# Seven-product matmuls of the second block: four products in one PSUM chain, sets interleaved by two products, scratch loads into idle weight pages

## The chip, the cores and the metric

One core of one Trainium2 chip runs the whole program: a gated attention block and, behind it, a second block with a short convolution and a SwiGLU. The metric is device microseconds (us) of one execution. Three runs of the kernel before gave 2760.71, 2763.57 and 2766.59 us.

## The reference, cut to what matters

Only the second block is touched. `x` is 1024 tokens by 1024 features; everything is float32.

```python
def short_conv_mixer(h, w_in, conv_w, w_out, on_grid):
    gate_b, gate_c, hv = jnp.split(h @ w_in, 3, axis=-1)
    u = gate_c * hv
    conv = conv3_grid(u, conv_w) if on_grid else conv3_seq(u, conv_w)
    return (gate_b * conv) @ w_out

def swiglu(h, w_in, w_out):
    gate, up = jnp.split(h @ w_in, 2, axis=-1)
    return (jax.nn.silu(gate) * up) @ w_out

x = x + g1 * short_conv_mixer(modulate(rmsnorm(x, norm1_g), sh1, sc1), ...)
x = x + g2 * swiglu(modulate(rmsnorm(x, norm2_g), sh2, sc2), ffn_w_in, ffn_w_out)
return rmsnorm(x, final_g)
```

`h @ conv_w_in` is 1024x1024 by 1024x3072, `@ conv_w_out` 1024x1024 by 1024x1024, `@ ffn_w_in` 1024x1024 by 1024x5632, `@ ffn_w_out` 1024x2816 by 2816x1024.

## The kernel before, in words

**Seven products.** Each of the four matrix products is done by Strassen's scheme in Winograd's form: operands in two by two blocks, seven block products P1 to P7 in place of eight, and sums before and after. Each float32 operand is split into a rounded half `hi` and a rest `lo` (line 106, a cast on ScalarE, then line 107, a subtraction on VectorE), and a block product is hi·hi + hi·lo + lo·hi. For four blocks of 128 of the contraction that makes 12 matmuls of 128x512, called a product below.

**Into features (`seven`, lines 1266 to 1291).** The tokens are the right operand. Seven forms of them (B11, B21, B12, T1 to T4) lie split in seven slots of `H` (slots 0 to 4) and `HB` (slots 5 and 6). A *set* is 128 features of each of two column blocks of the weight: `left_operands` (1195) loads two 512 KB tiles through the ring of raw tiles (four buffers, `next_raw`; line 1215), forms the sums on VectorE (1233 to 1238) and splits them into the ring of four weight pages `W` (`w_177` to `w_180`) and one half of `PA`. A set has four PSUM banks, and the next set the other four. ScalarE copies P1 out of its bank (1273), P2 is then added to P1 in the bank, P3 to P5 and P4 to P7, and VectorE makes five additions that read PSUM (lines 1280, 1282, 1284, 1288, 1290). The convolution has 12 sets, the SwiGLU 22 (NFF); for four of the first five of the one and the first six of the other, P1 and P2 were made in advance (`ahead`, 1258) while the tokens were still being prepared. Called *late* here are the 24 other sets.

**Out of features (`out_products`, 1352).** The roles turn: the left operand is the features' forms (TC or TF, stored to DRAM scratch by `spill`, 1294), the right one the weight (P1, P2, P4) or sums of its blocks (P3, P5, P6, P7; `sums_steps`, 1316, makes them on GpSimd with loads and stores, one step or more after each set: `mix.tick`). All operands are loaded 512 KB at a time through the raw tiles and split into pages of the token slots, which are free by then. A product name covers four token groups t = 0 to 3 in four banks; P1, P2, P5, P3 use banks 0 to 3, the others 4 to 7. After each name `conv_use` (1505) or `ffn_use` (1586) takes the four banks over.

**Between the two.** `third` (1485) is called by the conv's P4 for tokens t and by P3 for tokens 4 + t: it normalizes (1493), transposes on TensorE through PSUM (1404), stores and reloads half of it, and makes the SwiGLU's seven token forms (`right_operands`, 1173). It takes two or three raw tiles per call. At the very end `fourth` (1579) normalizes and stores the output; the lines 1605 to 1618 belong to the last two product names.

**What sets the order.** Each engine runs its instructions in one order, and that is set when the program is built, by a list scheduler that follows the program's order and a simulated timeline. The DMA issues of SyncE are in such an order too, so a load that waits for a raw tile holds up those queued behind it.

Of the kernel before, what the change touches and what calls it, by code (L numbers as in the profile page):

```python
# [27 lines left out]
def program(tc, I, out):  # L28
# [4 lines left out]
    with ctx:  # L33
# [1110 lines left out]
        def U(i, n=1):  # L1144
            return E[:, i * 512:(i + n) * 512]
# [13 lines left out]
        ORDER = ("P1", "P6", "P5", "P7", "P2", "P3", "P4")  # L1159
# [40 lines left out]
        def left_operands(w, c1, c2):  # L1200
# [3 lines left out]
            st = dict(i=i, bank=4 * (i % 2), w={})  # L1204
# [8 lines left out]
            def load(c):  # L1213
# [4 lines left out]
            def half(p, o):  # L1218
                return [p.r[:, q * 1024 + o:q * 1024 + o + 512].rearrange("p (k n) -> p k n", k=4) for q in range(2)]

            def first(keep=True):
                r = load(c1)
                if keep:
                    st["r"] = r, load(c2)
                p = page()
                split(p.r[:, 0:1024], p.r[:, 1024:2048], p.f[:, 0:1024], r)
                st["w"].update(P1=half(p, 512), P2=half(p, 0))

            def rest():
                r1, r2 = st["r"] if "r" in st else (load(c1), load(c2))  # L1230
                split(pa[:, 0:512], pa[:, 512:1024], paf[:, 0:512], r2[:, 0:512])
                a11, a12, a21, a22 = r1[:, 0:512], r1[:, 512:1024], r2[:, 0:512], r2[:, 512:1024]
                V.tensor_tensor(a21, a22, a21, ALU.add)
                V.tensor_tensor(a22, a12, a22, ALU.subtract)
                p = page()
                split(p.r[:, 0:1024], p.r[:, 1024:2048], p.f[:, 0:1024], r2)
                V.tensor_tensor(a12, a21, a12, ALU.subtract)
                V.tensor_tensor(a11, a11, a12, ALU.subtract)
                q = page()
                split(q.r[:, 0:1024], q.r[:, 1024:2048], q.f[:, 0:1024], r1)  # L1240
                st["w"].update(P5=half(p, 0), P7=half(p, 512), P3=half(q, 0), P6=half(q, 512),
# [24 lines left out]
        def seven(st, where, units, c12):  # L1266

            early = "c11" in st
            if not early:
                st["first"]()  # L1270
                st["p1"] = units.get()
# [399 lines left out]
```

## Time and profile before

| | |
|---|---|
| three runs, median (lowest to highest) | 2763.57 us (2760.71 to 2766.59) |
| the profiled execution: time, span | 2762.01 us, 2760.2 us |
| mean granted TensorE clock in it | 0.969 |
| matmuls on TensorE, busy | 13582, 2575.8 us (93%) |
| VectorE, ScalarE, GpSimd busy | 1922.2, 1067.2, 652.1 us |
| the chain that ended last, by engine | PE 71%, DVE 10%, DMA 9%, ACT 4% |

PE is TensorE, DVE VectorE, ACT ScalarE, POOL GpSimd, SP SyncE, which issues the DMAs. The busy shares are means over the whole span. What a part of the change is worth must be read in its own stage, by what TensorE waits for there. The second block's stages are: the convolution's products into features, 1677 to 1895 us; out of features, 1895 to 1970; the transition with `third`, 1970 to 2085; the SwiGLU's products into features, to 2509; out of features, to 2737; and the tail without any matmul to 2760.2.

### The profile page before, as it was taken

What the parts mean: (1) busy time and instruction counts of PE and PEld (TensorE: products, weight loads), DVE (VectorE), ACT (ScalarE), POOL (GpSimd) and SP (SyncE); (2) the same over time, 40 slices, a digit from 0 to 9 for tenths busy, and PEclk for the clock granted to TensorE, in tenths of its full rate; (3) what the DMA queues carried; (4) which work ended last, traced back from release to release, by engine and by line L of the source; (5) the groups of instructions that cost most, each with busy time, mean ns of one, the idle gap of its engine ahead of it and who ended that gap; (6) DMA issues with size and microseconds to landing.
All of it is one profiled execution on the core that took longest, in us unless ns stands there. A gap on an engine that the chain in (4) does not pass through costs nothing.

```text
span 2760.2 us, 36848 instructions
## 1 busy us (share of the span) xinstructions
PE 2575.8 (93%) x13582; PEld 2202.0 (80%) x13582; DVE 1922.2 (70%) x3097; ACT 1067.2 (39%) x1887; POOL 652.1 (24%) x638
## 2 busy tenths in 40 slices
PE   8999999999999999999999968999677998999976
PEld 5799998879999778888898856777556786888865
DVE  5677776667778764556778958786766887775536
ACT  4333334323233544355557853223442222224333
POOL 2100000010003304123447740240221445210012
PEclk9999999999999999999999989999788999999988
DMA  7454343555445336442543233465533677426645
GB/s 257 145 143 118 97 127 122 153 168 156 127 117 153 124 113 198 153 133 71 194 156 123 92 118 96 129 221 172 178 114 108 197 245 233 156 96 212 197 143 175
DMA packets 336937, 416.44 MB, mean 151 GB/s; under 512 B 17830, under 2 KB 200638, under 8 KB 336242
## 3 DMA queue, kind: packets, MB, share of 16 engines
q1 hardware_dynamic: 329012, 403.08, 46.1%
q10 hardware_dynamic: 7744, 11.01, 1.1%
q8 instruction: 106, 1.74, 0.3%
q14 instruction: 75, 0.61, 0.1%
HBM read 320.12 MB, written 93.91 MB: 150 GB/s over the span
## 4 chain that ended last, share of the span: by engine, by line
PE 71%; DVE 10%; DMA 9%; ACT 4%; issue 3%; POOL 3%; SPq 0%; DVEq 0%; POOLq 0%; ACTq 0%
PE PS L516 16%; PE PS L1254 14%; PE PS L1376 8%; PE PS L603 7%; PE PS L676 5%; PE PS L392 5%; PE PS L1053 3%; PE PS L998 2%; PE PS L861 2%; PE PS L895 2%; PE PS L883 2%; DVE w L107 1%; PE PS L497 1%; DMA E<-in_ffn_w_out 1%; DMA raw<-in_a_w_in 1%
## 5 line engine op out<-in xcount | busy, mean ns | idle before, releaser
L1254 PE MATMUL PS<-H,w 128*128 128x512 f32 x1776 | 432.5, 400 | 42.5 <-ACT w L106 21.7
L1254 PEld LDWEIGHTS PS<-H,w 128*128 128x128 f32 x1776 | 340.9, 193 | 123.8 <-ACT w L106 25.9
L106 ACT CAST w<-raw 128x1024 fp32r<-128x1024 f32 x202 | 211.1, 1050 | 509.5 <-PE PS L1254 134.4
L107 DVE TENSOR_TENSOR w<-raw,w 128x1024 fp32r<-128x1024 f32 x200 | 268.0, 1344 | 138.7 <-ACT w L106 138.3
L516 PE MATMUL PS<-H,w 128*128 128x320 f32 x2112 | 320.5, 309 | 1.3 <-DVE TT L525 1.3
L516 PEld LDWEIGHTS PS<-H,w 128*128 128x128 f32 x2112 | 310.8, 188 | 3.3 <-DVE TT L525 1.5
L1376 PE MATMUL PS<-H 128*128 128x512 f32 x924 | 220.1, 397 | 29.7 <-ACT H L106 29.7
L107 DVE TENSOR_TENSOR H<-raw,H 128x1024 fp32r<-128x1024 f32 (+1 forms) x133 | 165.0, 1248 | 117.8 <-ACT H L106 115.4
L1376 PEld LDWEIGHTS PS<-H 128*128 128x128 f32 x924 | 176.9, 192 | 69.6 <-ACT H L106 30.9
L106 ACT CAST H<-raw 128x1024 fp32r<-128x1024 f32 (+1 forms) x133 | 134.1, 1018 | 212.0 <-DMA raw<-in_a_w_in 71.3
L339 POOL TENSOR_TENSOR H<-ACC,H 128x256 fp32r<-128x256 f32 x52 | 50.6, 973 | 609.7 <-ACT H L338 483.4
L1254 PE MATMUL PS<-HB,w 128*128 128x512 f32 x672 | 169.5, 404 | 23.0 <-ACT E L1273 13.2
L1254 PEld LDWEIGHTS PS<-HB,w 128*128 128x128 f32 x672 | 127.0, 191 | 58.6 <-ACT E L1273 14.4
L320 DVE SCALAR_TENSOR_TENSOR ACC<-raw,CO,ACC 128x512 f32<-128x512 f32 x182 | 134.3, 750 | 20.7 <-DMA raw<-in_ada_w 18.1
L516 PE MATMUL PS<-H 128*128 128x320 f32 x960 | 144.7, 309 | 0.0
L516 PEld LDWEIGHTS PS<-H 128*128 128x128 f32 x960 | 141.1, 188 | 0.5
L603 PE MATMUL PS<-w,H 128*128 128x512 f32 x600 | 140.0, 391 | 0.0
L107 DVE TENSOR_TENSOR PTR<-PS,PTR 128x512 fp32r<-128x512 f32 x176 | 106.2, 613 | 35.0 <-ACT PTR L106 33.7
L603 PEld LDWEIGHTS PS<-w,H 128*128 128x128 f32 x600 | 111.5, 188 | 23.3
L392 PE MATMUL PS<-H 128*128 128x512 f32 x510 | 120.9, 391 | 0.0
L870 ACT ACTIVATE s<-s,sm 128x641 f32<-128x641 f32 (+1 forms) x128 | 103.3, 807 | 42.3 <-DVE sm L868 41.7
L106 ACT CAST PTR<-PS 128x512 fp32r<-128x512 f32 x176 | 91.8, 524 | 54.4 <-PE PS L883 49.8
(342 smaller groups left out, 4881.2 us busy)
## 6 DMA issues: line engine op xcount, KB each, us to landing
raw<-in_a_w_in SPq DMA_DIRECT2D x96, 512.0 KB
raw<-in_ada_w SPq DMA_DIRECT2D x80, 512.0 KB
raw<-in_ffn_w_in SPq DMA_DIRECT2D x50, 512.0 KB
E<-in_ffn_w_out SPq DMA_DIRECT2D x66, 256.0 KB
raw<-in_a_w_out SPq DMA_DIRECT2D x32, 512.0 KB
raw<-in_conv_w_in SPq DMA_DIRECT2D x28, 512.0 KB
TFT<-E SPq DMA_DIRECT2D x44, 256.0 KB
SFS<-E SPq DMA_DIRECT2D x44, 256.0 KB
```

What stands on the lines that cost most here:

```text
L106: A.copy(hi, src)
L107: turn["split"] = (eng or V).tensor_tensor(lo, src, hif, ALU.subtract)
L320: V.scalar_tensor_tensor(ACC[:, s, :], r[:, j, :], CO[:, c, k:k + 1], ACC[:, s, :], ALU.mult, ALU.add)
L392: T.matmul(ps, HT[0][:, k, ap, t * 128:(t + 1) * 128], w[:, k % 2, :], start=k == 0 and n == 0, stop=k == 7 and n == 2)
L516: T.matmul(pss[h][:, 0:320], w[:, k, :], HT[0][:, k, ap, h * 320:(h + 1) * 320], start=k == 0 and n == 0, stop=k == 7 and n == 2)
L603: turn["mm"] = T.matmul(accs[t], ys[j].r[:, ap * 640 + t * 128:ap * 640 + (t + 1) * 128], wv[:, j, :], start=kp == 0 and j == 0 and n == 0 ...
L676: T.matmul(pss[j], HP[0][:, g + j, k, ap, :], w[:, k % 2, :], start=k == 0 and n == 0, stop=k == 7 and n == 2)
L861: T.matmul(PF[:, c0:c0 + m], q, k[:, part, :], start=part == 0, stop=part == 1)
L870: A.activation(out=p[:, :nk + 1], in_=p[:, :nk + 1], func=AF.Exp, scale=-1.0, bias=sm[:, j:j + 1], accum_out=sm[:, 2 + j:3 + j])
L1053: T.matmul(ps, w[:, k, :], HP[0][:, 2 + 4 * tg:6 + 4 * tg, k, ap, :], start=k == 0 and n == 0, stop=k == 7 and n == 2)
L1254: turn["mm"] = T.matmul(ps, w[:, k, :], b[:, ap, k, :], start=start and k == 0 and n == 0, stop=k == 3 and n == 2, skip_group_check=not start)
L1376: turn["mm"] = T.matmul(ps[:, t], x[ap][:, i, t * 128:(t + 1) * 128], s[v][:, i, :], start=new and j + i == 0 and q == 0, stop=j + i == nj ...
```

## The change

1. **Chain.** In a late set P1, P6, P5 and P3 are accumulated in one PSUM bank in this order. ScalarE copies the running sum out after P1, after P6 and after P5 (after.py lines 1283 and 1302), and the sum after P3 is read where it is used. P2 has a bank of its own, and P7 and P4 share one. VectorE adds only P2, P7 and P4 (1284, 1306, 1312): three additions, not five. Early sets keep five.
2. **Overlap.** `run_sets` issues the next set's left operands and its P1 and P2 ahead of this set's P3 and P4.
3. **Half loads.** Each 512 KB load of a left operand becomes two of 256 KB, grouped so that the sums need fewer buffers at a time.
4. **Out of features** the names go P1, P2, P6, P7, P5, P4, P3, with P1, P6, P5, P3 chained in banks 0 to 3 and P2, P7, P4 in banks 4 to 7; the uses change accordingly (1550 to 1556). P3's extra addition goes, and in `ffn_use` eight GpSimd operations go (before.py lines 1614 and 1615).
5. **Landing.** Scratch loads (all feature forms, and the weight sums of P3, P5, P6, P7) no longer take raw tiles: for the convolution they land in the two pages of slot 4 (weight pages 10 to 8), for the SwiGLU in the `W` pages, four and eight landing places. Raw tiles then carry only direct weight loads and the tiles of `third` and of x.

```diff
-            st = dict(i=i, bank=4 * (i % 2), w={})
+            st = dict(i=i, w={})
...
+            def two(x, y):
                 r = next_raw()
-                SY.dma_start(r.rearrange("p (k n) -> p k n", k=8), rows(w, c, 128))
+                for q, src in enumerate((x, y)):
+                    SY.dma_start(r[:, q * 512:(q + 1) * 512].rearrange("p (k n) -> p k n", k=4), src)
                 return r
...
-                ps = PS[:, st["bank"] + {"P1": 0, "P2": 0, "P6": 1, "P5": 2, "P3": 2, "P7": 3, "P4": 3}[name]]
+                ps = PS[:, st["i"] % 2 + {"P1": 0, "P6": 0, "P5": 0, "P3": 0, "P2": 2, "P7": 4, "P4": 4}[name]]
...
+        def run_sets(sets, where, units):
...
+                    A.copy(c11, product(st, "P1", where))
+                    V.tensor_tensor(c11, product(st, "P2", where), c11, ALU.add)
...
+                def chain(dst, ps):
+                    if early:
+                        V.tensor_tensor(dst, ps, U(st["p1"]), ALU.add)
+                    else:
+                        A.copy(dst, ps)
+                chain(u2, product(st, "P6", where, early))
+                d = product(st, "P7", where)
+                chain(u3, product(st, "P5", where, False))
+                V.tensor_tensor(u3, d, u3, ALU.add)
+                if nxt:
+                    nxt["rest"]()
+                    head(nxt)
+                c12 = product(st, "P3", where, False)
+                d = product(st, "P4", where, False)
+                V.tensor_tensor(u2, d, u2, ALU.add)
...
-        def out_products(w, nj, right, sums, pages, use):
+        def out_products(w, nj, right, sums, pages, raws, use):
+
+            inner = ring(raws)
...
-            for name in ("P1", "P6", "P2", "P7", "P5", "P4", "P3"):
-                ps = PS[:, 0:4] if name in ("P1", "P2", "P5", "P3") else PS[:, 4:8]
-                new = name in ("P1", "P6", "P7", "P5")
+            for name in ("P1", "P2", "P6", "P7", "P5", "P4", "P3"):
+                ps = PS[:, 4:8] if name in ("P2", "P7", "P4") else PS[:, 0:4]
+                new = name in ("P1", "P2", "P7")
...
-                    return wpage(x, n, 512), wpage(moving(name, j, n), n, 512)
+                    x = wpage(x, n, 512, raw=inner())
+                    s, raw = moving(name, j, n)
+                    return x, wpage(s, n, 512, raw=raw)
...
+        def out_use(name, t, ps):
+
+            u2, u3, r = U(t), U(4 + t), U(8 + t)
+            if name in ("P1", "P6"):
+                A.copy(u2, ps)
+            elif name == "P2":
+                V.tensor_tensor(r, ps, u2, ALU.add)
+                G.tensor_tensor(r, r, gbs[0], ALU.mult)
+            elif name == "P5":
+                A.copy(u3, ps)
+                V.tensor_tensor(u3, PS[:, 4 + t], u3, ALU.add)
+                G.tensor_tensor(u3, u3, gbs[1], ALU.mult)
+            return u2, u3, r
...
-                G.tensor_tensor(u2, u2, gbs[0], ALU.mult)
-                G.tensor_tensor(r, r, u2, ALU.add)
-            else:
+            elif name == "P3":
```

Three places show how the order moved.

TensorE where the convolution's products out of features end and `third`'s transposes (L1404, now L1434, reading a raw tile) begin; L1376, now L1406, is a matmul of `out_products`. Before:

```order
L1376 MATMUL PS<-H 128x512 x72
L1404 MATMUL PS<-ident,raw_181 128x128 x4
L1404 MATMUL PS<-ident,raw_13954 128x128 x4
L1404 MATMUL PS<-ident,raw_181 128x128 x4
L1404 MATMUL PS<-ident,raw_13954 128x128 x4
L1404 MATMUL PS<-ident,raw_181 128x128 x4
L1404 MATMUL PS<-ident,raw_13954 128x128 x4
L1404 MATMUL PS<-ident,raw_181 128x128 x4
L1404 MATMUL PS<-ident,raw_13954 128x128 x4
L1376 MATMUL PS<-H 128x512 x6
L1376 MATMUL PS<-HB 128x512 x6
```

and now, the last rows of P4, then P3:

```order
L1406 MATMUL PS<-H 128x512 x4
L1406 MATMUL PS<-HB 128x512 x12
L1406 MATMUL PS<-H 128x512 x4
L1406 MATMUL PS<-HB 128x512 x6
L1406 MATMUL PS<-H 128x512 x41
L1434 MATMUL PS<-ident,raw_13954 128x128 x4
L1406 MATMUL PS<-H 128x512 x4
L1434 MATMUL PS<-ident,raw_181 128x128 x4
L1406 MATMUL PS<-H 128x512 x13
L1434 MATMUL PS<-ident,raw_13954 128x128 x4
L1434 MATMUL PS<-ident,raw_181 128x128 x4
L1434 MATMUL PS<-ident,raw_13954 128x128 x4
```

The 48 matmuls of P3 stood behind the transposes of the first four token groups (the rows of 6 by turns with `H` and `HB`); now all of them but 17 stand ahead of the first transpose, and the rest among the first ones.

TensorE in a late SwiGLU set (L1254, now L1265; `w_177` to `w_180` and `PA` are the pages of the left operand, `H` or `HB` the slot of the right one; `HB` is P2 or P3, `PA` is P4). Before:

```order
L1254 MATMUL PS<-H,PA 128x512 x12
L1254 MATMUL PS<-H,w_179 128x512 x12
L1254 MATMUL PS<-H,w_177 128x512 x12
L1254 MATMUL PS<-H,w_180 128x512 x24
L1254 MATMUL PS<-HB,w_179 128x512 x12
L1254 MATMUL PS<-HB,w_177 128x512 x12
L1254 MATMUL PS<-H,PA 128x512 x12
L1254 MATMUL PS<-H,w_178 128x512 x12
```

and now:

```order
L1265 MATMUL PS<-H,w_180 128x512 x12
L1265 MATMUL PS<-HB,w_178 128x512 x12
L1265 MATMUL PS<-H,PA 128x512 x12
L1265 MATMUL PS<-H,w_180 128x512 x12
L1265 MATMUL PS<-H,w_177 128x512 x12
L1265 MATMUL PS<-H,w_178 128x512 x12
L1265 MATMUL PS<-HB,w_178 128x512 x12
L1265 MATMUL PS<-H,w_179 128x512 x4
L1265 MATMUL PS<-HB,w_177 128x512 x12
L1265 MATMUL PS<-H,PA 128x512 x12
```

Before, P2 and P3 of a set followed one another. Now the rows read, with n for a set: P6 of n+1, P3 and P4 of n, P7 and P5 of n+1, P1 and P2 of n+2, four matmuls of P6 of n+2, then P3 and P4 of n+1. Between two links of a chain there are three products (P6 to P5), two (P5 to P3) and one (P1 to P6).

VectorE in the early SwiGLU sets, which TensorE takes two at a time before and now, from the last product of set 0 to the operands of sets 2 and 3. L107 is a split; the sums of a set's left operands are L1233 to L1238 (now L1244 to L1249) and are made in place behind the split into `PA`, which wants that half of `PA` free, so behind P4 of two sets earlier; L1290 (now L1312) adds P4, L1558 and L1559 (now L1602 and L1603) belong to the gate. Before:

```order
L1290 TENSOR_TENSOR E<-PS,E 128x512
L1558 SCALAR_TENSOR_TENSOR E<-E 128x512
L107 TENSOR_TENSOR PA<-raw_183,PA 128x512
L1559 SCALAR_TENSOR_TENSOR E<-E 128x512
L1233 TENSOR_TENSOR raw_183<-raw_183 128x512
L1288 TENSOR_TENSOR E<-PS,E 128x512
L1234 TENSOR_TENSOR raw_183<-raw_13954,raw_183 128x512
L1237 TENSOR_TENSOR raw_13954<-raw_183,raw_13954 128x512
L1558 SCALAR_TENSOR_TENSOR E<-E 128x512
L1290 TENSOR_TENSOR E<-PS,E 128x512
L1238 TENSOR_TENSOR raw_13954<-raw_13954 128x512
L107 TENSOR_TENSOR w_180<-raw_183,w_180 128x1024
```

and now (two of L1249 and the first page's split, `w_178`, come next):

```order
L1312 TENSOR_TENSOR E<-PS,E 128x512 x2
L107 TENSOR_TENSOR PA<-raw_183,PA 128x512
L107 TENSOR_TENSOR PA<-raw_182,PA 128x512
L1603 SCALAR_TENSOR_TENSOR E<-E 128x512 x2
L1244 TENSOR_TENSOR raw_183<-raw_183,raw_13954 128x512
L1244 TENSOR_TENSOR raw_182<-raw_182,raw_181 128x512
L1602 SCALAR_TENSOR_TENSOR E<-E 128x512
L1245 TENSOR_TENSOR raw_13954<-raw_13954 128x512
L1245 TENSOR_TENSOR raw_181<-raw_181 128x512
L1603 SCALAR_TENSOR_TENSOR E<-E 128x512
L1246 TENSOR_TENSOR raw_13954<-raw_183,raw_13954 128x512
L1246 TENSOR_TENSOR raw_181<-raw_182,raw_181 128x512
```

Set 2's sums stood ahead of set 1's addition of P4, which is the second L1290. Now both additions of P4 stand first, and the sums of sets 2 and 3 follow by turns.

At the program's end five of P3's splits stood behind the first use of P4 (L1607) on VectorE; now all of them stand ahead of it (L1645). In the convolution's first three sets (two early, one late) P3 now follows P5 in the same bank at once, behind four other matmuls, and at once.

## Rows read from the trace of the kernel before

**Rows 1.** The page: span, then busy time, share and instructions of two engines.

```profile
span 2760.2 us, 36848 instructions
...
PE 2575.8 (93%) x13582; PEld 2202.0 (80%) x13582; DVE 1922.2 (70%) x3097; ACT 1067.2 (39%) x1887; POOL 652.1 (24%) x638
```

**Rows 2.** Windows by stage; the columns stand in the first row.

```profile
core 0: us, PE busy (x) PEld busy (x) DVE busy (x) ACT busy (x) POOL busy (x), PEclk, DMA share, GB/s
...
1677.00:1895.00 218.00, 208.03 (x898) 167.81 (x899) 176.40 (x208) 48.77 (x57) 46.63 (x28) 1.00 0.43 137
1895.00:1970.00 75.00, 70.81 (x303) 57.33 (x301) 44.69 (x49) 26.18 (x31) 13.63 (x10) 0.98 0.60 190
1970.00:2085.50 115.50, 66.74 (x256) 48.72 (x256) 74.39 (x127) 54.88 (x111) 22.00 (x20) 0.73 0.43 143
2085.50:2210.00 124.50, 116.06 (x471) 91.92 (x472) 95.83 (x114) 31.59 (x40) 37.04 (x22) 0.95 0.51 163
2210.00:2509.00 299.00, 286.28 (x1238) 232.91 (x1237) 228.14 (x250) 81.12 (x105) 97.64 (x62) 0.98 0.56 181
2509.00:2658.50 149.50, 149.49 (x659) 123.25 (x657) 73.37 (x74) 53.22 (x59) 9.81 (x7) 1.00 0.58 187
2658.50:2737.00 78.50, 63.28 (x264) 51.54 (x264) 42.14 (x45) 29.77 (x42) 19.41 (x17) 0.89 0.59 184
2737.00:2760.20 23.20, 0.00 (x0) 0.00 (x0) 18.21 (x34) 5.05 (x14) 8.50 (x9) 0.57 0.44 159
```

**Rows 3.** Timeline of TensorE: start, us, operation, [idle before, what ended it].

```profile
1913.13 11.60 PE L1376 MATMUL PS<-H 128*128 128x512 f32 x42 [3.93 <-ACT H L106]
...
2003.83 3.33 PE L1376 MATMUL PS<-H 128*128 128x512 f32 x6 [11.68 <-ACT H L106]
...
2085.50 19.42 PE L1254 MATMUL PS<-H,w 128*128 128x512 f32 x72 [10.89 <-ACT w L106]
...
2118.59 7.57 PE L1254 MATMUL PS<-H,w 128*128 128x512 f32 x32 [1.40 <-ACT w L106]
...
2160.77 1.19 PE L1254 MATMUL PS<-H,w 128*128 128x512 f32 x4 [1.27 <-ACT w L106]
...
2344.22 7.35 PE L1254 MATMUL PS<-HB,w 128*128 128x512 f32 x24 [11.60 <-ACT E L1273]
...
2672.57 14.01 PE L1376 MATMUL PS<-H 128*128 128x512 f32 x48 [14.08 <-ACT H L106]
```

**Rows 4.** Groups by line, 1640 to 2760 us: a split, an addition of PSUM, the copy.

```profile
L107 DVE TENSOR_TENSOR w<-raw,w 128x1024 fp32r<-128x1024 f32 x100 | 133.8, 1344 | 51.9 <-ACT w L106 51.8
...
L1282 DVE TENSOR_TENSOR E<-PS,E 128x512 f32<-128x512 f32 x34 | 23.4, 688 | 10.9 <-PE PS L1254 7.8 <-DMA TFT<-E 1.9 <-issue 0.2
...
L1273 ACT COPY E<-PS 128x512 f32<-128x512 f32 x24 | 14.1, 586 | 59.3 <-PE PS L1254 31.1 <-DMA TFT<-E 9.4 <-POOL E L1303 8.7
```

**Rows 5.** Timelines of SP and VectorE in the transition.

```profile
1990.89 1.67 SPq L121 DMA_DIRECT2D raw<-TCB  x2
...
2010.09 0.69 DVE L1532 TENSOR_TENSOR E<-PS,E 128x512 f32<-128x512 f32 x1 [1.90 <-PE PS L1376]
...
2016.22 0.74 DVE L1493 TENSOR_SCALAR raw<-E,RM 128x1024 f32<-128x1024 f32 x1
```

**Rows 6.** Timeline of GpSimd ahead of the wait at 2344 us.

```profile
2339.31 1.71 POOL L1301 TENSOR_TENSOR E<-E 128x512 f32<-128x512 f32 x1
```

**Rows 7.** Timelines of SP and ScalarE between P5 and P4 of the SwiGLU.

```profile
2666.66 0.38 SPq L121 DMA_DIRECT2D raw<-in_ffn_w_out  x1
...
2671.47 1.04 ACT L106 CAST H<-raw 128x1024 fp32r<-128x1024 f32 x1 [1.28 <-DMA raw<-in_ffn_w_out]
```

**Rows 8.** Timeline of VectorE in the last 30 us.

```profile
2732.41 0.69 DVE L1607 TENSOR_TENSOR E<-PS,E 128x512 f32<-128x512 f32 x1 [4.76 <-POOL E L1606]
...
2751.68 0.68 DVE L1617 TENSOR_TENSOR E<-PS,E 128x512 f32<-128x512 f32 x1
```

**Rows 9.** Waits, 1677 to 2737 us: total, times, longest.

```profile
ACT w L106 <- DVE raw L1238: 63.5, 15, 14.0
```

More of the change, by code (lines that the diff above doesn't have):

```diff
@@ L1221, in first, with half, loads @@
+            def half(p, o, step=1024):
+                return [p.r[:, q * step + o:q * step + o + 512].rearrange("p (k n) -> p k n", k=4) for q in range(2)]
+            def loads():
+                if "x" not in st:
+                    st["x"], st["y"] = two(load(c1, 1), load(c2, 1)), two(load(c2, 0), load(c1, 0))
             def first(keep=True):
-                r = load(c1)
+                p = page()
                 if keep:
-                    st["r"] = r, load(c2)
-                p = page()
@@ L1226, in first @@
[L1226 to L1237, printed above, removed]
+                    loads()
@@ new lines, in first, with rest @@
+                    for q, src in enumerate((st["x"][:, 0:512], st["y"][:, 512:1024])):
+                        o = q * 512
+                        split(p.r[:, o:o + 512], p.r[:, 1024 + o:1536 + o], p.f[:, o:o + 512], src)
+                else:
+                    split(p.r[:, 0:1024], p.r[:, 1024:2048], p.f[:, 0:1024], two(load(c1, 1), load(c1, 0)))
+                st["w"].update(P1=half(p, 0), P2=half(p, 512))
+            def rest():
+                loads()
+                x, y = st["x"], st["y"]
+                a12, a22, a21, a11 = x[:, 0:512], x[:, 512:1024], y[:, 0:512], y[:, 512:1024]
+                split(pa[:, 0:512], pa[:, 512:1024], paf[:, 0:512], a21)
+                V.tensor_tensor(a21, a21, a22, ALU.add)
+                V.tensor_tensor(a22, a12, a22, ALU.subtract)
+                V.tensor_tensor(a12, a21, a12, ALU.subtract)
+                p = page()
+                split(p.r[:, 0:1024], p.r[:, 1024:2048], p.f[:, 0:1024], x)
@@ new lines, in gated_up, with use @@
+        def gated_up(f):
+            def use(c11, c12, c21, c22, free):
+                y = []
+                for x1, x2 in ((c11, c21), (c12, c22)):
+                    y.append(units.get())
+                    s1 = U(y[-1])
+                    A.activation(out=s1, in_=x1, func=AF.Tanh, scale=0.5)
+                    V.scalar_tensor_tensor(s1, s1, 1.0, x1, ALU.add, ALU.mult)
+                    V.scalar_tensor_tensor(s1, s1, 0.5, x2, ALU.mult, ALU.mult)
+                free()
+                ys.append(y)
+                if f % 2:
+                    spill(TF, f // 2, *((U(a), U(b)) for a, b in ys), units)
+                    units.put(*ys[0], *ys[1])
+                    ys.clear()
+                if f == 5:
+                    mix.begin(sums(f_out, NFF // 2, SF, [units.get() for _ in range(4)]), NFF - 7)
+                mix.tick()
+            return use
@@ L1569, in program @@
+        sets = [(first[f] if f < 6 else left_operands(f_in, f * 128, (NFF + f) * 128), gated_up(f)) for f in range(NFF)]
+        run_sets(sets, N3, units)
         mix.end()
@@ L1620, in ffn_use @@
                 fourth(4 + t, [r, u3])
[L1622 removed]
+        out_products(f_out, NFF // 2, TF, SF, slot_pages((0, 4, 3, 1, 6, 5, 2)),
+                     [p.f[:, q * 1024:(q + 1) * 1024] for p in W for q in range(2)], ffn_use)
 def constants():
```

163 lines of the change are left out of this document (62 added, 101 removed).

## The prediction

> **What bounds the kernel now.** I read the page first: TensorE is busy for 93% of the span [rows 1], so the change can give back only what TensorE idles in the stages it touches. The windows by stage show where that is [rows 2]: span less PE busy is 10.0 us in the convolution's products into features, 4.2 us in those out of features, 48.8 us in the transition, 8.4 us in the SwiGLU's first 125 us, 12.7 us in its rest, nothing for the next 149.5 us, 15.2 us around P5 and P4, and 23.2 us in the tail, 122.5 us in all. One product of 12 matmuls lasts 149.5 / 659 x 12 = 2.72 us at full clock. The timeline of TensorE then names the long single waits [rows 3]: operands that are cast late (1913, 2003, 2085, 2672) and one P1 copy (2344). VectorE stands behind the small ones: busy for 176 of 218 us in the first stage and for 96 of 124.5 in the fourth.
>
> The sum is made against the profiled execution, 2762.0 us. The median of the three runs is 1.6 us above it, and I add that at the end. About 0.2%, 5.5 us, is what a measurement of this kernel can tell from no change.
>
> **Convolution into features: -2.** Eight late sets lose two additions of 0.688 us each [rows 4], 11.0 us of VectorE's 176; ScalarE, busy for 49 of 218 us, gets two copies of 0.586 us per set. About half of the 10.0 us should go with that: -5. Against it, P3 follows P5 in one bank in the first three sets with four matmuls or none between, so TensorE waits for the copy or the addition that reads the bank, about 0.7 us and what VectorE has begun: 3 x 1.0 = +3. Bounds: -8 and +5.
>
> **Convolution out of features: -2.** The wait of 3.93 us at 1913 is for feature forms that the last `spill` has just stored. The new order has P2's matmuls to run there, but the spill is no earlier behind the last set. Bounds: -4 (it goes) and +4 (it doubles).
>
> **Transition: -16.** P4 of the convolution ends about 1970, where the 48.8 us begin. P3's loads could be issued only at 1990.89, when `third` gave raw tiles back [rows 5]; TensorE ran P3 from 2003.83 [rows 3]. VectorE's first use of P3 came at 2010.09, and the normalization of token group 4 at 2016.22 [rows 5], 46 us behind P4. In the new order P3's operands land in pages that `third` does not use, and 31 of its 48 matmuls precede the first transpose. They take 4 x 2.72 = 10.9 us behind P4, so P3's uses could start some 30 us sooner. What is late next is `third` for groups 0 to 3, which holds the raw tiles until the loads above went out, about 1991, and some us more; group 4 takes its tiles from that ring. So group 4 starts near 1998 in place of 2016: 18 us. The steps from there to the steady run at 2085.5, the 10.89 us of waiting at its end included [rows 3], stay. I take 16, since VectorE's 74 us of the 115.5 are pressed together. Bounds: -25 (the clock, 0.73 there, comes back sooner too) and -8 (half).
>
> **SwiGLU, early sets: +10.** This is the term against the change. The idle time is 8.4 us, and early sets keep five additions, so there is little to gain. But the order of VectorE now puts the sums of sets 2 and 3 behind both additions of P4. Behind the second one stand 14 operations (two splits into `PA`, four of the gate, eight sums) and a split of 1.344 us; at the 0.688 us of the additions [rows 4] that is 0.7 + 9.6 + 1.3 = 11.6 us until set 2's first operand is whole, and TensorE has nothing else in its order. Before, the sums ran beside P3 and P4 of set 1, and such a place cost 1.40 us at 2118 and 1.27 us at 2160 [rows 3], some 2 to 4 us with the small waits behind them. From sets 2 and 3 to 4 and 5 the order is by turns and one product covers some: (12 x 0.688) + 1.3 - 2.7 = 6.9 us. So 11.6 + 6.9, less the 8.4 us of now, all put to such places: +10. Bounds: -2 (the loads and casts set the place as before) and +14.
>
> **SwiGLU, rest: 0.** The wait of 11.60 us is a P1 copy that wants a unit which a `spill` holds; GpSimd came to that spill only at 2339.31 [rows 6], because it walks through the weight sums first. The number of these steps is unchanged. P5 of a set now wants the unit nine products after the set before it, where the copy came eleven later: 2 x 2.72 = 5.4 us less room, but the overlap starts the row of sums two products earlier. Bounds: -12 (it goes) and +8 (it comes twice, partly). Elsewhere this stage has no idle time; TensorE covers the additions saved.
>
> **P5 to P4: -2.** TensorE waited 14.08 us for P4's operands and then took 14.01 us for 48 matmuls [rows 3], 3.1 us above 4 x 2.72, at a lower granted clock (0.89 over the stage, between its two levels 1.2 and 2.4 GHz). P4's weights were issued at 2666.66 and cast at 2671.47 [rows 7], behind the raw tiles that the P5 use holds and behind a load of the feature form. Now the form is already in its page and the weights go first, some 1.2 us earlier and with one load less beside them; one more copy of 0.586 us stands ahead of the P5 use. Bounds: -3 and +3. The wait and most of the slow clock stay.
>
> **Tail: -10.** 23.2 us without matmuls [rows 2]. P4 ended at 2672.57 + 14.01 + 7 x 2.72 = 2705.6, but its use for group 2 stood at 2732.41 [rows 8], because P3's splits were among the uses of groups 0 and 1 and the x tiles of groups 2 and 3 follow their stores. P3's last use came at 2751.68 [rows 8], 14.7 us behind the last matmul. Now the splits stand ahead of P4's uses, which fit into P3's run of 11 x 2.72 = 29.9 us; the eight GpSimd operations go as well. From P3's last use to the end it was 8.5 us; that stays, and with 4 to 5 us of backlog the tail becomes 13 us. Bounds: -14 (no backlog) and -3.
>
> **The chain's copies: +4.** A link may not run before ScalarE has copied the bank: one product, 2.72 us, between P1 and P6 of a late SwiGLU set, two or three elsewhere. The copy takes 0.586 us, but ScalarE's queue is in order, and a cast ahead of it waited for VectorE 15 times for 63.5 us, 4.2 us each, at most 14.0 us [rows 9]. A mean wait leaves 4.2 + 0.6 - 2.7 = 2.1 us for TensorE; at two such places I get 4. Bounds: 0 and +10. Queued behind the copy are the next casts, and TensorE waits for those again. The Trainium skill ("PSUM — Partial Sum Buffer", Summary: rules for kernel authors) says to read another bank than the one that matmuls are writing. By it these waits would be the price in every set; no row before shows a link that waited for a copy, apart from the unit at 2344.
>
> The half loads add 78 issues of 0.38 us [rows 7], 30 us of SP's queue over some 870 us. What hides them is that the queue mostly stands at waits for raw tiles; without that cover they would delay a first load by 0.4 us each. I take nothing.
>
> **Sum.** -2 - 2 - 16 + 10 + 0 - 2 - 10 + 4 = -18, so 2744.0 us, and with 1.6 us for the median 2745.6 us. The half-widths of the bounds as independent errors (6, 4, 8, 8, 10, 3, 5, 5) give a root of 18 us: 2728 to 2764 for this case alone.
>
> **Rivals.**
> 1. *The transition does not shorten.* Groups 4 to 7 are held by raw tiles and VectorE, not by P3. For it: 74 us of VectorE there and four raw tiles at up to three per call. Against it: the first P3 use waited 1.90 us for TensorE with VectorE idle [rows 5]. Without that term: 2761.6 us, within 0.2%. Chance 0.10.
> 2. *The chain waits in each late set (slower).* The place is P6 behind P1. If the copy stands behind a late cast in all 24 late sets at the 2.1 us above, it costs 50 us in place of 4: 2791.6 us. The sign turns at (18 + 4) / 24 = 0.9 us per set. For it: the 63.5 us of waits [rows 9] lie in this queue. Against it: ScalarE is busy for a quarter of these stages [rows 2] and most links have two products or more. The skill's rule above is this case. Chance 0.10, of it 0.02 near 0.9 us per set.
> 3. *The early sets do not wait.* The sums come late for another reason in both kernels, and the term is -2: 2733.6 us; if the wait at 2344 goes as well, 2721.6. For it: before, such places already ended with casts that wait. Against it: the order of VectorE is fixed. Chance 0.18.
> 4. My forecast: chance 0.62. Some 0.04 of it lies within 0.2% of no change.
>
> Faster by over 0.2%: 0.58 + 0.18 + 0.01 (rival 1's better half) = 0.77; same 0.04 + 0.09 + 0.02 = 0.15; slower 0.08. The range runs from the third rival's lower case to the upper end of the forecast's own, which leaves out the second: 2721 to 2764 us.
>
> **What would show it.** Right: P3 of the convolution runs straight behind P4, and group 4 is normalized 15 to 20 us sooner behind it; two waits of TensorE, about 10 and 6 us, lie between the pairs of early SwiGLU sets; the last use of P3 comes about 5 us behind the last matmul; 10 us or more remain between P5 and P4. Wrong: TensorE waits for the copies at 1283 or 1302 in most late sets, the spill's wait appears more than once, or loads become late between P1 and P5 of the SwiGLU's second product, where no idle time was.

## The result and the profile after

The changed kernel takes 2734.93 us (median of four runs, 2730.57 to 2738.98), against 2765.08 us (2760.71 to 2766.64) for the kernel before beside it. The ratio is 0.9893, 95% interval 0.9873 to 0.9914: faster by 30 us, where I forecast 18. The profiled execution took 2736.48 us, 25.5 us below that of before; the account below closes on these 25.5 us.

The page of the kernel after has the same matmuls, busy for 5.0 us longer [rows 1]. VectorE lost 44 us of work and ScalarE got 31, since additions became copies:

```profile
span 2734.7 us, 37065 instructions
...
PE 2580.8 (94%) x13582; PEld 2205.6 (81%) x13582; DVE 1878.4 (69%) x3053; ACT 1097.8 (40%) x1975; POOL 665.2 (24%) x638
```

Both kernels issue as many matmuls in each stage, so points with equal counts can be compared. Three stretches close the sum: from the span's start to the steady SwiGLU (the 72 matmuls at 2085.50 in [rows 3], at 2065.28 now), from there to the end of P5 out of features (2364 matmuls), and from there to the span's end (264).

| us | to steady SwiGLU | to P5's end | to the span's end | span |
|---|---|---|---|---|
| before | 2085.5 | 573.0 | 101.7 | 2760.2 |
| after | 2065.3 | 588.8 | 80.6 | 2734.7 |
| difference | -20.2 | +15.8 | -21.1 | -25.5 |

The change thus earned 41 us and gave 16 back. Windows by stage of the kernel after (columns in the first row; to the conv's end, transition, SwiGLU to P5, rest):

```profile
core 0: us, PE busy (x) PEld busy (x) DVE busy (x) ACT busy (x) POOL busy (x), PEclk, DMA share, GB/s
1677.00:1969.60 292.60, 281.84 (x1200) 227.75 (x1201) 219.54 (x241) 93.73 (x122) 68.72 (x42) 0.98 0.49 158
1969.60:2065.25 95.65, 61.94 (x257) 46.42 (x255) 68.40 (x122) 50.61 (x107) 22.65 (x20) 0.82 0.44 150
2065.25:2656.40 591.15, 558.03 (x2364) 451.47 (x2364) 371.79 (x417) 191.32 (x265) 160.51 (x97) 0.97 0.56 185
2656.45:2735.00 78.55, 63.73 (x264) 51.25 (x264) 46.11 (x71) 25.70 (x48) 16.85 (x16) 0.90 0.41 141
```

The convolution ends where it did, 1969.6 against 1970 [rows 2]. Within it TensorE idles for some 3 us less and its matmuls are busy for 3.0 us longer (281.84 for 208.03 + 70.81), at a granted clock of 0.98 where the first of the two stages had 1.00. The transition takes 95.7 us where it took 115.5, at a granted clock of 0.82, not 0.73. In the SwiGLU the same 2364 matmuls are busy for 558.0 us; in the same stretch of before they were busy for 551.8 us of 573.1, at a granted clock of 0.98. So of the 15.8 us lost there 6.2 are slower matmuls and 9.6 are idle time (30.8 us, for 21.2, up to P5's end at 2654.12). Timeline of TensorE in the kernel after (start, us, operation, in brackets idle before and what ended it):

```profile
1924.03 12.79 PE L1406 MATMUL PS<-H 128*128 128x512 f32 x48 [2.29 <-ACT H L106]
...
2065.28 19.46 PE L1265 MATMUL PS<-H,w 128*128 128x512 f32 x72 [12.17 <-ACT w L106]
...
2104.82 18.44 PE L1265 MATMUL PS<-H,w 128*128 128x512 f32 x72 [8.90 <-ACT w L106]
...
2139.64 10.94 PE L1265 MATMUL PS<-H,w 128*128 128x512 f32 x40 [4.58 <-ACT w L106]
2154.20 7.54 PE L1265 MATMUL PS<-H,w 128*128 128x512 f32 x20 [3.62 <-DVE E L1300]
...
2208.73 5.74 PE L1265 MATMUL PS<-H,w 128*128 128x512 f32 x24 [2.76 <-ACT E L1302]
...
2298.37 8.04 PE L1265 MATMUL PS<-H,w 128*128 128x512 f32 x24 [6.04 <-ACT E L1302]
...
2656.49 1.20 PE L1406 MATMUL PS<-H 128*128 128x512 f32 x4 [2.37 <-ACT H L106]
2659.42 7.51 PE L1406 MATMUL PS<-H 128*128 128x512 f32 x20 [1.74 <-DVE H L107]
2668.12 11.20 PE L1406 MATMUL PS<-H 128*128 128x512 f32 x48 [1.19 <-ACT H L106]
...
2722.30 0.85 PE L1406 MATMUL PS<-H 128*128 128x512 f32 x3
```

The waits at 2104, 2139 and 2154, 17.1 us, stand where [rows 3] has 1.40 and 1.27 us, with the small ones beside them 7.5 us. The wait for a unit (a buffer that the sets' results pass through) of 11.60 us is now two, of 2.76 and 6.04 us, as ScalarE's timeline shows: both times it stood idle until a spill's store (`TFT<-E`) was done, for an activation of the gate, and the copy that TensorE waits for is queued behind that activation.

```profile
2207.57 0.63 ACT L1601 ACTIVATE E<-E 128x512 f32<-128x512 f32 x1 [12.59 <-DMA TFT<-E]
2208.11 0.57 ACT L1302 COPY E<-PS 128x512 f32<-128x512 f32 x1
...
2297.21 0.63 ACT L1601 ACTIVATE E<-E 128x512 f32<-128x512 f32 x1 [17.79 <-DMA TFT<-E]
2297.75 0.57 ACT L1302 COPY E<-PS 128x512 f32<-128x512 f32 x1
```

Between P5 and P4 the 14.08 us in one piece are three pieces of 5.3 us together, with 24 matmuls of P3 between them.

The forecast's places on VectorE (timeline: group 4's normalization, the boundary between the first and second pair of early sets, P3's last use):

```profile
1997.80 0.74 DVE L1533 TENSOR_SCALAR raw<-E,RM 128x1024 f32<-128x1024 f32 x1
...
2095.74 1.29 DVE L1312 TENSOR_TENSOR E<-PS,E 128x512 f32<-128x512 f32 x2
2096.95 1.28 DVE L107 TENSOR_TENSOR PA<-raw,PA 128x512 fp32r<-128x512 f32 x2
...
2102.96 1.29 DVE L1246 TENSOR_TENSOR raw<-raw,raw 128x512 f32<-128x512 f32 x2
...
2725.74 0.69 DVE L1653 TENSOR_TENSOR E<-PS,E 128x512 f32<-128x512 f32 x1
```

Group 4 is normalized at 1997.80, 18.4 us sooner than in [rows 5]. The pair's splits and sums run from 2096.95 on, and the cast that TensorE waits for stands right behind the first L1246 in ScalarE's timeline (first row; the second is the first weight cast of P4):

```profile
2103.73 3.89 ACT L106 CAST w<-raw 128x1024 fp32r<-128x1024 f32 x4 [4.23 <-DVE raw L1246]
...
2667.02 1.04 ACT L106 CAST H<-raw 128x1024 fp32r<-128x1024 f32 x1 [2.06 <-DMA raw<-in_ffn_w_out]
```

### The profile page after: what moved, and what is told of

Its sections match the earlier page's. It is cut to its first block, busy times and chain, and to the rows that moved or that the text cites. A ratio compares the mean times of both kernels' runs of the same rounds, so it can differ in the third digit from the quotient of the medians.

```text
span 2734.7 us, 37065 instructions
## 1 busy us (share of the span) xinstructions
PE 2580.8 (94%) x13582; PEld 2205.6 (81%) x13582; DVE 1878.4 (69%) x3053; ACT 1097.8 (40%) x1975; POOL 665.2 (24%) x638
## 5 line engine op out<-in xcount | busy, mean ns | idle before, releaser
L1265 PE MATMUL PS<-H,w 128*128 128x512 f32 x1776 | 442.8, 406 | 70.7 <-ACT w L106 36.0
L1265 PEld LDWEIGHTS PS<-H,w 128*128 128x128 f32 x1776 | 346.0, 196 | 157.4 <-ACT w L106 40.2
L106 ACT CAST w<-raw 128x1024 fp32r<-128x1024 f32 (+1 forms) x226 | 214.2, 959 | 428.9 <-DMA raw<-in_a_w_in 127.2
L107 DVE TENSOR_TENSOR w<-raw,w 128x1024 fp32r<-128x1024 f32 (+1 forms) x224 | 284.4, 1283 | 125.8 <-ACT w L106 125.5
L1406 PE MATMUL PS<-H 128*128 128x512 f32 x924 | 218.9, 396 | 7.6 <-ACT H L106 5.9
L1406 PEld LDWEIGHTS PS<-H 128*128 128x128 f32 x924 | 176.0, 191 | 46.8 <-ACT H L106 7.1
L1265 PE MATMUL PS<-HB,w 128*128 128x512 f32 x672 | 170.6, 402 | 5.3 <-DVE E L1300 3.5
L1265 PEld LDWEIGHTS PS<-HB,w 128*128 128x128 f32 x672 | 127.7, 191 | 38.0 <-ACT E L1272 2.7
L107 DVE TENSOR_TENSOR PTR<-PS,PTR 128x512 fp32r<-128x512 f32 x176 | 106.3, 613 | 34.7 <-ACT PTR L106 33.3
L107 DVE TENSOR_TENSOR H<-raw,H 128x1024 fp32r<-128x1024 f32 x68 | 90.6, 1337 | 42.7 <-ACT H L106 38.5
L106 ACT CAST H<-raw 128x1024 fp32r<-128x1024 f32 x68 | 70.6, 1043 | 109.0 <-DMA raw<-in_a_w_in 67.6
```

Source lines behind the costliest of these rows:

```text
L106: A.copy(hi, src)
L107: turn["split"] = (eng or V).tensor_tensor(lo, src, hif, ALU.subtract)
L1265: turn["mm"] = T.matmul(ps, w[:, k, :], b[:, ap, k, :], start=start and k == 0 and n == 0, stop=k == 3 and n == 2, skip_group_check=not start)
L1406: turn["mm"] = T.matmul(ps[:, t], x[ap][:, i, t * 128:(t + 1) * 128], s[v][:, i, :], start=new and j + i == 0 and q == 0, stop=j + i == nj ...
```

## The experiments

The theory after the result: the landing earns the time at both ends; chain, overlap and half loads lose it between them, through VectorE's order at the pairs. All ratios are against the kernel before on the same chip. The three stretches are those of the table above, from the profiled execution of each kernel. They are not so matched: the runs come from several chips, on which the kernel before took 2755.84 to 2765.08 us, so a few us between two rows count only where a wait shows them. No run has the chain alone or the overlap alone.

| run | median us | ratio, 95% interval | to steady | to P5's end | to the end |
|---|---|---|---|---|---|
| old_sets | 2725.90 | 0.9876, 0.9859 to 0.9893 | 2063.4 | 581.1 | 79.7 |
| landing_only | 2725.49 | 0.9877, 0.9855 to 0.9898 | 2067.0 | 571.0 | 86.4 |
| no_landing | 2773.77 | 1.0052, 1.0034 to 1.0070 | 2086.8 | 589.0 | 98.2 |
| whole_loads | 2730.95 | 0.9901, 0.9881 to 0.9920 | 2068.6 | 579.2 | 80.5 |
| sums_first | 2722.07 | 0.9872, 0.9851 to 0.9892 | 2061.9 | 583.1 | 79.5 |
| halves | 2726.60 | 0.9885, 0.9863 to 0.9907 | 2061.3 | 578.1 | 87.0 |
| spill_dve | 2715.14 | 0.9844, 0.9825 to 0.9863 | 2063.5 | 564.6 | 86.5 |
| double_copy | 2751.00 | 0.9983, 0.9973 to 0.9993 | 2072.1 | 594.4 | 81.0 |
| p3_behind | 2735.32 | 0.9926, 0.9912 to 0.9939 | 2069.2 | 573.3 | 92.6 |

Three more, x_units, best and best_chain, have no break at P5's end to read and follow below.

**The landing alone.** The kernel before, with its scratch loads moved to the pages of the new one:

```diff
-                    return wpage(x, n, 512), wpage(moving(name, j, n), n, 512)
+                    x = wpage(x, n, 512, raw=inner())
+                    s, raw = moving(name, j, n)
+                    return x, wpage(s, n, 512, raw=raw)
```

> The kernel before with nothing changed but the landing of scratch loads (slot 4's pages, then the W pages). My theory: 2765 - 20 (transition) - 8 (P5 to P4) - 10 or more (tail) = 2727 us or less, 0.986 of before, and 24 matmuls of P3 stand ahead of P4 in the SwiGLU's second product. Rival: the wait between P5 and P4 and the tail need the new order of the names, ScalarE's copies and the eight GpSimd operations less: the 14 us stay, the tail gives half, 2765 - 20 - 6 = 2739 us.

Measured: 0.9877. Its windows (SwiGLU to P5, rest) and TensorE's timeline:

```profile
2066.94:2639.75 572.81, 551.73 (x2364) 448.11 (x2364) 406.84 (x444) 172.05 (x210) 147.86 (x93) 0.98 0.57 191
2639.75:2724.00 84.25, 64.29 (x264) 51.59 (x264) 51.64 (x70) 25.98 (x49) 29.04 (x24) 0.88 0.39 131
```

```profile
2066.96 19.36 PE L1254 MATMUL PS<-H,w 128*128 128x512 f32 x72 [9.36 <-ACT w L106]
...
2318.69 7.33 PE L1254 MATMUL PS<-HB,w 128*128 128x512 f32 x24 [8.32 <-ACT E L1273]
...
2651.73 12.82 PE L1380 MATMUL PS<-H 128*128 128x512 f32 x48 [2.70 <-ACT H L106]
...
2707.53 0.85 PE L1380 MATMUL PS<-H 128*128 128x512 f32 x3
```

The transition's gain (-18.5) and 15.3 of the 21.1 us at the end are there, the loss between them is not: TensorE is busy for 551.7 us, as before. Of the 15.3 us, 6.9 lie between P5's end and the last matmul and 8.3 behind it. The whole net gain of the change is had by this part alone.

**The change without the landing.** Everything else of it, with the scratch loads back in raw tiles:

```diff
-                    x = wpage(x, n, 512, raw=inner())
+                    x = wpage(x, n, 512)
```

> The changed kernel with all scratch loads through the raw tiles again (ten pages for the convolution). My theory: the early sets still lose about 14 us and nothing is won in the transition or between P5 and P4; a few us may be won in the tail by the fewer operations: 2765 + 14 - 4 = 2775 us, slower than before. Rival: the chain and the overlap win by themselves in the late sets and the tail: 2750 us or less.

Measured: slower, 1.0052. Steady SwiGLU at 2086.8, and TensorE's timeline has the pair's wait and the long wait ahead of P4 again:

```profile
2125.42 4.80 PE L1265 MATMUL PS<-H,w 128*128 128x512 f32 x14 [8.89 <-ACT w L106]
...
2690.81 13.07 PE L1405 MATMUL PS<-H 128*128 128x512 f32 x48 [15.02 <-ACT H L106]
```

So the two parts of the change act on different stretches and roughly add up: this kernel has the changed kernel's 589 us between them and ends near those of before (2086.8 for 2085.5, 98.2 for 101.7). By spans, -35.8 for the landing alone and +13.8 for the rest make -22.0, where the change has -25.5.

**Old sets.** The changed kernel (landing and new order out of features) with the sets of before: whole loads, four banks, five additions, no overlap. It is the kernel before with the landing and the new order; one line of its edit against before:

```diff
-            for name in ("P1", "P6", "P2", "P7", "P5", "P4", "P3"):
+            for name in ("P1", "P2", "P6", "P7", "P5", "P4", "P3"):
```

> The changed kernel with the sets of the kernel before (whole loads, four banks per set, no overlap, no chain); landing and the new order out of features stay. My theory: the two waits between pairs of early SwiGLU sets (8.9 and 4.6 us at 2105 and 2140 in the changed kernel, with a wait of 3.6 us behind them) are made by the new order of the sets, and the 20 us of the transition, the 8 us between P5 and P4 and the 13 us of the tail come from the landing. So about 14 us come off: 2721 us, 0.984 of before, with no wait over 3 us between the early sets and the P1 copy waiting about 11 us for the spill again. Rival: the waits there are only moved from elsewhere, or the chain earns as much in the late sets as the early ones lose: 2735 us or more.

Measured: 0.9876, level with the landing alone, and not the 0.984 of my theory: against the change (0.9893) the intervals overlap, and the stretch to P5's end gives back 7.7 us (581.1 for 588.8), not 14. The waits did as expected: none between the early sets is over 1.6 us, and the P1 copy waits for the spill again, 3.02 and 8.76 us. Against the landing alone the new order out of features gives 6.7 us behind P5 (79.7 for 86.4), 4.8 of them behind the last matmul, and 10.1 us are lost ahead of it; the medians see neither. So of the 17.8 us by which the change is longer than the landing alone in that stretch, 10.1 come without chain, overlap and half loads. They are idle time (7.4) and slower matmuls (2.7); why is open.

**Whole loads.** The change with 512 KB loads, and with the order of sums of before, which splits the first page behind two sums and not three:

```diff
-                for q, src in enumerate((x, y)):
-                    SY.dma_start(r[:, q * 512:(q + 1) * 512].rearrange("p (k n) -> p k n", k=4), src)
+                SY.dma_start(r.rearrange("p (k n) -> p k n", k=8), rows(w, c, 128))
```

> The changed kernel with whole 512 KB loads of the left operands (two of 256 KB each before). My theory: these loads are hidden, 2735 us within 4. Rival, the Trainium skill's rule that larger DMAs are better (DMA: Bandwidth & Descriptors, rules for kernel authors): 5 us or more faster. Second rival: the finer halves let raw tiles go sooner, so whole loads are 5 us or more slower.

Measured: 0.9901, no difference from 0.9893. But the pair's wait of 8.9 us went, and another came elsewhere in TensorE's timeline:

```profile
2247.09 1.22 PE L1253 MATMUL PS<-HB,w 128*128 128x512 f32 x2 [8.12 <-ACT w L106]
```

**Half loads alone.** The landing with half loads and their order of sums, the edit just shown the other way round.

> The landing alone (0.988 of before) with half loads of the left operands added, no chain and no overlap. My theory: the waits between the pairs are neither the half loads' nor the chain's alone, but come when both P4 additions stand ahead of the next sums; here VectorE keeps the second behind the next PA split, so at most 4 us between pairs and the time of the landing alone within 5 us. Rival: the half loads, with four sums ahead of the first page in place of two, make the wait by themselves: 8 us or more slower than the landing alone.

Measured: 0.9885, as the landing alone. The pair's wait is 1.42 and 2.19 us; in its place TensorE waits for additions later on, the longest being

```profile
2306.96 5.49 PE L1266 MATMUL PS<-H,PA 128*128 128x512 f32 x12 [6.84 <-DVE E L1296]
```

So the 8.9 us belong to no single part: they need the new sets and the half loads, with their order of sums, together. My reading is that each combination gives the list scheduler another order.

**VectorE's order at the pairs.** The change, with the sums of sets 2 and 4 issued ahead of the P4 addition of the set before:

```diff
-                V.tensor_tensor(u2, d, u2, ALU.add)
+                with tc.issue_after(turn["split"].ins) if stagger and n in (1, 3) else nullcontext():
+                    V.tensor_tensor(u2, d, u2, ALU.add)
```

> The changed kernel with one thing more: in the early SwiGLU sets VectorE makes the sums and splits of set 2 (and 4) ahead of set 1's (3's) addition of P4, and the split of set 3's (5's) PA behind them. My theory, that VectorE's order makes the two waits: 8.9 us at 2105 becomes 3 to 5, 4.6 us at 2140 2 to 4, and the time 2735 - 8 = 2727 us. Rival: something else is late there (loads, a weight page, the half of PA) and the waits stay within 2 us of what they were.

Measured: 0.9872; the interval overlaps that of the change, so the 6 us between them are not shown by the medians. The trace shows that VectorE's order makes a good part of these waits: in place of 8.90, 4.58 and 3.62 us the longest in the early sets are now 5.41, 1.91 and 1.15.

```profile
2098.12 2.07 PE L1266 MATMUL PS<-H,w 128*128 128x512 f32 x4 [5.41 <-ACT w L106]
```

**The spill on VectorE.** The landing, with the four subtractions of `spill` on VectorE:

```diff
-            G.tensor_tensor(t1, b22, b21, ALU.subtract)
+            V.tensor_tensor(t1, b22, b21, ALU.subtract)
```

> The landing alone with the four subtractions of each spill on VectorE in place of GpSimd. My theory: the P1 copy's wait for a unit (11.6 us at 2344 before, 8.3 us at 2319 with the landing alone) is GpSimd's queue of weight sums ahead of the spill; it goes: 8 us less than the landing alone, 0.985 of before. Rival: VectorE's 44 operations more (30 us) come out as waits for its additions in the SwiGLU, and the time is that of the landing alone or more.

Measured: 0.9844, some 9 us below the landing alone, with intervals that just overlap. The unit's wait shrinks from 8.32 to 4.77 us and doesn't go, so GpSimd's queue [rows 6] was one part of it; what holds the rest is open.

```profile
2308.48 7.41 PE L1254 MATMUL PS<-HB,w 128*128 128x512 f32 x24 [4.77 <-ACT E L1273]
```

**The x tiles in units.** The landing, with the x tiles of the P5 use in free units, not raw tiles:

```diff
-                x = next_raw()[:, 0:512]
+                x = U(12 + t)
```

> The landing alone with the x tiles of the SwiGLU's P5 use in four free units in place of raw tiles. My theory: P4's weights queue behind these raw tiles; they now load while P5 runs, so the wait before P4's matmuls (2.7 us behind the 24 matmuls of P3, at a lower clock after it) goes, and the waits of 1.9 and 1.6 us ahead of those shrink: 5 us less than the landing alone, 0.986 of before. Rival: GpSimd and ScalarE between P5 and P4 are the limit, not the loads: no change.

Measured: 2716.37 us, 0.9849 (0.9830 to 0.9868), with an interval that just overlaps that of the landing alone. TensorE's timeline shows no wait any more from 2492 us to its last matmul: P4's weights had been waiting for raw tiles that x held.

**P3 behind P4.** The landing, with the first 24 matmuls of P3 held behind P4's:

```diff
-                    for t in range(4):
-                        one(j, n, x, s, t)
+                    with tc.issue_after(turn["mm"].ins) if name == "P3" and nj > 4 and j == 0 else nullcontext():
+                        for t in range(4):
+                            one(j, n, x, s, t)
```

> The landing alone, with the first 24 matmuls of P3 in the SwiGLU's second product kept behind P4's last on TensorE. My theory: they are what shortened the wait between P5 and P4, so one wait of 12 to 14 us comes back ahead of P4, its first 48 matmuls take about 14 us, and the time is 6 to 8 us above the landing alone (0.990 of before). Rival: P4's operands come sooner by themselves, the wait is 8 us or less and the time is within 3 us of the landing alone.

Measured: 0.9926, 0.0049 or 13 us above the landing alone. Behind P5's end, where the edit acts, it is 6.2 us (92.6 for 86.4), as forecast; no wait shows the rest of the 13. In TensorE's timeline the wait is back in one piece, with slower matmuls behind it, as in [rows 3]; the granted clock over the 48 is 0.79, for 0.87 in the landing alone:

```profile
2656.11 13.96 PE L1380 MATMUL PS<-H 128*128 128x512 f32 x48 [13.63 <-ACT H L106]
```

The 48 matmuls start as late behind P5 in both kernels (13.63 us, and 13.8 in the landing alone). So the hole is worth the 24 matmuls that are done in it, 2 x 2.72 = 5.4 us, and 1.1 us on the 48.

**The copies twice.** The change, with each of the chain's copies of a late set made a second time into the same unit; two of the three:

```diff
                     else:
+                        A.copy(dst, ps)
                         A.copy(dst, ps)
```

> The changed kernel with each of ScalarE's three copies of a late set made twice: 72 copies more, 42 us of ScalarE's time. My theory: a copy is on TensorE's path at a few places only, so 2735 + 0 to 6 us. Rival, the case that I gave a chance of 0.15 and that the Trainium skill's rule (PSUM — Partial Sum Buffer) stands for: each late set waits for a copy between links, and twice the copy costs at least 24 x 0.59 = 14 us.

Measured: 0.9983, 0.0090 or 25 us above the change by the ratios, and 12.8 us by the spans of the two profiled executions (2747.5 for 2734.7), in which the chip of this run has its part: the kernel before took 9 us less there. My theory, 0 to 6 us, fell by either; so did the mechanism of the rival (whose chance stood at 0.10 in the prediction, not 0.15). TensorE's waits from 1677 to 2720 us (total, times, longest), in the kernel after and then in this one:

```profile
PE PS L1265 <- ACT w L106: 31.5, 9, 12.2
PE PS L1265 <- ACT E L1302: 9.7, 4, 6.0
```

```profile
PE PS L1265 <- ACT w L106: 32.2, 8, 9.6
PE PS L1265 <- ACT E L1305: 25.4, 4, 14.3
```

Twice the copies are 15.7 us more of waiting, and still in four places, not in each late set. The two long ones, 8.04 and 14.26 us at 2216 and 2307 where the change has 2.76 and 6.04, again stand behind a gate's activation for which ScalarE waited until a spill's store was done:

```profile
2214.65 0.63 ACT L1604 ACTIVATE E<-E 128x512 f32<-128x512 f32 x1 [16.24 <-DMA TFT<-E]
...
2305.90 0.63 ACT L1604 ACTIVATE E<-E 128x512 f32<-128x512 f32 x1 [17.62 <-DMA TFT<-E]
```

So 13.5 of the 15.7 us are the unit's wait grown longer. How the second copies lengthen it is open, and so is what else the ratio's 25 us hold.

**Both remedies.** `best` is the landing with the spill on VectorE and x in units; `best_chain` is the same two edits on the changed kernel, with VectorE's order at the pairs as in `sums_first`.

```diff
-            G.tensor_tensor(t1, b22, b21, ALU.subtract)
+            V.tensor_tensor(t1, b22, b21, ALU.subtract)
...
-                x = next_raw()[:, 0:512]
+                x = U(12 + t)
```

> The landing alone with the spill's subtractions on VectorE and the P5 use's x tiles in units, sets and order of names as before. The two gains lie in different stages and should add: 0.988 - 0.003 - 0.003 = 0.982 of before, about 2709 us. Rival: a spill that ends sooner only moves a wait to later sets, 0.985.

> The changed kernel (chain, overlap, half loads, new order of names) with the sums ahead in the early sets, the spill's subtractions on VectorE and the P5 use's x tiles in units. My theory: the chain and the overlap earn nothing that these do not, so 0.983 to 0.985 of before, not under the kernel with the sets of before beside it. Rival: with the other waits gone the two additions less per late set pay, and it is 3 us or more under that kernel.

Measured: 2709.94 us, 0.9832 (0.9817 to 0.9848), and 2708.98 us, 0.9831 (0.9818 to 0.9845). Both beat both kernels, by 46 us against before. Between them there is nothing that the runs can tell: with the landing and the two remedies in place, chain, overlap, half loads and the new order of names earn no time beyond the intervals, some 6 us.

## Why the prediction was right, and where it was not

The direction, the range and the mechanism of the greatest term, the transition, were right; the gain was 30 us by the medians and 25.5 in the profiles, not 18. Of the other terms some came near by luck. Step by step, in the profiled executions:

- **Convolution, forecast -4, measured 0.** P4 ends at 1969.6, as before. The idle time did shrink by some 3 us, and the wait at 1913 became one of 2.29 us at 1924; but the same matmuls were busy for 3.0 us longer, at a lower granted clock, and the forecast has no term for that.
- **Transition, forecast -16, measured -20.2.** The mechanism is as told: P3's operands no longer wait for raw tiles, its matmuls run straight behind P4, and group 4 comes at 1997.80, against 1998 in the forecast. Landing alone gives 18.5, and the kernel without it has its steady SwiGLU at 2086.8. Rival 1 fell with that.
- **SwiGLU with the copies, forecast +14, measured +15.8 to P5's end.** Early sets: the two waits at the pairs were forecast at 11.6 and 6.9 us and came as 8.90 and 8.20 (4.58 and 3.62); with 0.33 us beside them they are 17.4 us for 7.5, the +10 of the forecast. The first is shorter because the cast that TensorE waits for wants only 11 of the 14 operations that I counted, up to the first L1246, and because I had put each at its duration of 0.688 us: the ten from 2096.95 to 2102.96 start 0.60 us apart. Rest: the unit's wait of 11.60 became 8.80 in two places, and small waits grew by 2.6. Copies: the +4 for copies behind late casts did not show at all. What I left out is 6.2 us of slower matmuls, at a lower granted clock behind such waits. So the sum came out near by luck: a term that was not there stands for one that I did not have. Rival 3, no wait in the early sets, fell. A sign that I had named for being wrong, the spill's wait in more than one place, did come.
- **P5 to P4, forecast -2, measured -8.3.** This is the step that failed: "The wait and most of the slow clock stay." P4's own weights are as late as I said: cast at 2667.02, 12.9 us behind P5's end, where [rows 7] has 13.0. What I missed is that P3's operands come from scratch, so that they land in the idle pages without a raw tile; 24 matmuls of P3 run ahead of P4 in the hole. They were to be read in the order of TensorE's instructions: 132 matmuls from `H` stand ahead of the P4 and P3 rows with `HB`, where there were 108. The wait is 8.8 us less (5.3 for 14.08) and the 48 matmuls take 2.8 less (11.20 for 14.01); the 24 in the hole take 8.71 us, 3.3 more than 2 x 2.72. That makes the 8.3. Holding these matmuls back alone cost 6.2 us there and 13 by the medians.
- **Tail, forecast -10, measured -12.8.** The last use of P3 is at 2725.74, 2.6 us behind the last matmul, where I had allowed 4 to 5 us of backlog [rows 8]. From the last matmul to the end it is 24.4 us before, 16.0 with the landing alone and 11.6 now. So 8.3 of the 12.8 us are the landing's, which has neither the new uses nor the eight GpSimd operations less; I had put all to the order of the splits and to these operations. The new uses and the order of names give the other 4.5.
- **Rival 2, a wait for the copy in each late set, fell.** TensorE waits four times for a copy, 9.7 us, of which 8.80 are the two waits for a unit. The Trainium skill ("PSUM — Partial Sum Buffer", Summary: rules for kernel authors) advises reading another bank than the one that matmuls write. The chain reads the bank that its next link writes, and the trace shows no price of that per set: most links show no wait, and the long ones stand behind a store. Twice the copies cost time, but at these same two places.

-20.2 + 15.8 - 8.3 - 12.8 = -25.5.

The change's name tells of its chain first. The runs say that chain, overlap and half loads together earn nothing that the medians show, and that the landing earns all of the gain. Taking 44 us of work off VectorE moved next to no time, since TensorE had hardly been waiting for that work. In the kernel before its waits for such additions, from 1677 to 2720 us (total, times, longest), were

```profile
PE PS L1254 <- DVE E L1282: 4.3, 5, 1.7
...
PE PS L1254 <- DVE E L1284: 1.5, 1, 1.5
```

## What to carry to other kernels

A small ring that carries both loads with early operands and loads that wait for a late consumer makes every user wait for the slowest; giving the loads from scratch idle pages of their own was worth 34 us here, and the x tiles out of the ring, with the spill on VectorE, another 12 (0.9832 for 0.9877). When a wait ends on a copy, read what stands ahead of that copy in its engine's queue: here it was an activation that waited for a store. When a wait ends on something late, look for independent work whose operands are already there: 24 matmuls in the hole were worth 6.2 us by the trace and 13 by the medians, 1.1 us of it through the clock that they kept up. A gain on an engine that nobody waits for is no gain, and a reordering that comes with it can cost more than its instructions.

## What I had not expected of the hardware

Matmuls behind a wait can cost time as well as the wait: 48 of them took 11.20, 12.82 and 13.96 us behind waits of 1.19, 2.70 and 13.63 us (the change, the landing alone, P3 behind P4), at granted clocks of 1.00, 0.87 and 0.79 over these stretches; 72 of them took 18.44 us at 0.89 behind the 8.90 us. It is not so behind each: the 24 behind the 2.76 us took 5.74, at 1.00. A forecast that counts waits alone misses this: 6.2 us of 15.8 in the SwiGLU, 3.0 in the convolution. VectorE starts such additions 0.60 us apart when each lasts 0.69. And a second copy of the same 586 ns [rows 4], on an engine that is busy for a third of the SwiGLU (191.3 of 591.2 us), cost 12.8 us by the spans and 25 by the ratios, through waits behind a store and not at the links.
